# A hybrid attention layer on one core: the ALiBi slope folded into q's norm weights, and the softmax rows divided on GpSimd

## The chip, the cores and the metric

The kernel runs on one core of a Trainium2 chip. The metric is the device time of one execution in microseconds (us). A core has five engines with a queue of instructions each: TensorE (PE in the profile, its weight loads PEld), VectorE (DVE), ScalarE (ACT), GpSimd (POOL) and SyncE (SP, which here only issues DMAs). Each engine runs its queue in order; between engines semaphores set the order. SBUF is the on-chip memory of 128 partitions, PSUM the accumulator memory that TensorE writes; GpSimd works on SBUF alone.

## The reference

One decoder layer on 512 tokens of width 1024. Two token mixers work side by side, then come an MLP and a gated embedding. The change touches the second mixer, softmax attention with 8 heads of 128. Queries and keys are normalised per head (`rms_norm` with a weight vector each), and a penalty that grows with the distance is taken from the scores:

```
slopes = 2.0 ** (-8.0 * arange(1, H + 1) / H)          # H = 8: 2^-1 ... 2^-8
qh = rms_norm(mq, moba_q_norm)
kh = rms_norm(mk, moba_k_norm)
sc = einsum('qd,kd->qk', qh, kh) * dh ** -0.5 - slope * abs(t - pos)
prob = softmax(where(visible, sc, -inf))
out = prob @ vh
```

With 512 tokens and blocks of 256 keys, a query sees all keys up to itself. The rest of the layer is: a gated linear attention (4 heads), output gates for both mixers, `x = x + y @ w_out`, an MLP with squared ReLU (4096 hidden features), and a gated per-layer embedding.

## The kernel before, in words

Activations stand feature-major, [128 features, 512 tokens]; weights are the stationary operand. A float32 product is three passes of TensorE on exact halves, hi*hi + hi*lo + lo*hi (`mm3`, lines 101 to 103). So each operand is split: ScalarE copies the high half, and VectorE or GpSimd subtracts it for the low half (`split`, L91 and L92, and `halves`, L151 and L153). Weights come in units of 512 KB by DMA and are split the same way: `whi` by ScalarE, `wlo` by VectorE at L153.

The program is written in the order of issue. The projections are cut into ticks of 12 matmuls. Work of the attention heads runs as generators in the background: at each tick every generator that is due emits one stage, which thus goes into each engine's queue between the projections' instructions. A `yield n` puts the next stage n ticks later, `yield 0` later in the same tick. Nothing reorders the queues afterwards.

The projection of queries and keys has 16 tiles of 128 features, q and k of 8 heads in turn, so a head takes four ticks. The result of a tile is scaled into `e` (L417) and normalised by `qk_norm`: squares and their split (ScalarE, and GpSimd at L403 for the low half `ql`), their mean over the partitions by TensorE (L275, L276), the inverse root by ScalarE and VectorE (L286, L287), then e times weight times root (L408, weight `gq` or `gk`), and the split of the result with its low half on GpSimd (L153 on POOL).

Five ticks after k, `attention` begins for the head: the slope times the distances (L425, tile `s`), the split of the values (GpSimd, L92), the scores of four tiles of 128 queries against 128, 256, 384 or 512 keys (TensorE, 1280 columns in all). `lower` (L441) turns a tile of scores in PSUM to slope * distance - score in SBUF and takes the minimum of each row; `soften` is the exponential with the row's sum on ScalarE (L445); `normalise` takes the reciprocal of the sum (L448) and multiplies the row by it (L449). One tick or two later TensorE transposes the rows (L475), which are split again (L486 on ScalarE, L491 or L153 on VectorE), and multiplied with the values into `ob`.

After the 16 tiles comes a short projection for the low-rank gate, whose result VectorE reads at L526, and the gated linear attention. Two PSUM banks (`acc`) take turns for the projections, six (`aux`) for the rest.

Of the kernel before, what the change touches and what calls it, by code (L numbers as in the profile page):

```python
"""Hybrid decoder layer on one NeuronCore: MoBA attention and gated linear attention in parallel,
gated branches, a squared-ReLU MLP and a gated per-layer embedding.

Activations are kept feature-major ([feature, token]), so that each projection is
out^T = W^T act^T with W as the stationary operand; only the two value projections are
token-major.  A float32 product runs as three fp32r products of exact halves: the tensor engine
carries 12 significant bits, x = hi + lo with both halves exact, and hi*hi + hi*lo + lo*hi.
The RMS factor of a token commutes with the projection that follows and is applied to its output.

The program is in the order of issue.  The projections are cut into ticks of 12 matmuls; the work  # L10
of the attention heads runs in the background as generators that emit a stage per tick, each
stage fed by stages of earlier ticks, so that the tensor engine finds its operands ready.
"""
# [14 lines left out]
P = 128  # L28
# [9 lines left out]
# columns of the packed per-feature vectors  # L38
C_MIX, C_MLP, C_PLE, C_ON, C_Q, C_K, C_B, NCOL = 0, 8, 16, 24, 32, 33, 34, 38

# feature-major tiles of w_in in the order of use: (q, k) of each MoBA head, (q, k) of each GLA
# head, then g_r, gate_a and gate_b
# [4 lines left out]
def kernel(ctx: ExitStack, tc: tile.TileContext, xT, pT, w_in, w_val, w_glr, w2, cols,  # L47
# [41 lines left out]
    def split(hi, lo, src, eng=None):  # L89
        """hi + lo = src, exactly."""  # L90
        A.activation(hi, src, AF.Copy)  # L91
        (eng or V).tensor_tensor(lo, src, f32(hi), ALU.subtract)  # L92

    def scaled_split(hi, lo, x, g):
        """hi + lo = x * g, g a column."""
        A.activation(hi, x, AF.Copy, scale=g)  # L96
        V.scalar_tensor_tensor(lo, x, g, f32(hi), ALU.mult, ALU.subtract)

    def mm3(ps, a, b, start=True, stop=True):
        """ps (+)= a^T b from exact halves a = (hi, lo), b = (hi, lo)."""  # L100
        PE.matmul(ps, a[0], b[0], start=start, stop=False)  # L101
        PE.matmul(ps, a[0], b[1], start=False, stop=False)  # L102
        PE.matmul(ps, a[1], b[0], start=False, stop=stop)  # L103

# [1 line left out]
    jobs = []  # L106

    def spawn(gen, wait=0):
        """gen yields the number of ticks until its next stage; 0 is later in the same tick, when
        the others' stages of the tick have been issued."""  # L110
        jobs.append([gen, wait])
# [43 lines left out]
    def low_rank(g1, g2, raw):  # L155
        # The low-rank gate takes two passes: its columns come in pairs of groups of 16, the
        # first for hi*hi + hi*lo and the second for lo*hi.  Their sum is left to the product
        # with w2, where three pairs carry hi*hi, lo*hi and hi*lo in one pass.
        g1, g2 = (g.rearrange("p k (n c) -> p k n c", c=16) for g in (g1, g2))
        for i in range(0, 8, 2):  # L160
            A.activation(g1[:, :, i], raw, AF.Copy)
            A.activation(g2[:, :, i], raw, AF.Copy)
        yield 0
        for i in range(0, 8, 2):
            V.tensor_tensor(g1[:, :, i + 1], raw, f32(g1[:, :, i]), ALU.subtract)
            V.tensor_scalar(g2[:, :, i + 1], raw, 0.0, None, ALU.mult)
# [13 lines left out]
    def gemm_fm(n, act, evac, nu=1):  # L180
        """n tiles of 128 output features, [128 features, 512 tokens], each over nu units of
        [128, 8 k-tiles, 128]; act(k) are the halves of the activations' k-tile."""
        for i in range(n):
            ps = bank(accp, "acc")
            for u in range(nu):
                w = ready.pop(0)
                for half in range(2):
                    for k in range(4 * half, 4 * half + 4):
                        mm3(ps, (w[0][:, k], w[1][:, k]), act(8 * u + k),
                            u == 0 and k == 0, u == nu - 1 and k == KT - 1)  # L190
                    if half:
                        convert()
                    tick()
            evac(i, ps)

    def gemm_tm(act, evac, first=None):
        """512 output features, [128 tokens, 512 features] for each of the four tiles of tokens,
        over four units of [128, 2 k-tiles, 512]."""
        ps = [bank(accp, "acc"), bank(accp, "acc"), bank(), bank()]
        for u in range(4):  # L200
            w = first(u) if first else ready.pop(0)
            order = [(k, m) for k in range(2) for m in range(NT)]
            if u == 3:
                order = [(k, m) for m in range(NT) for k in range(2)]
            for j, (k, m) in enumerate(order):
                a = act(2 * u + k)
                ms = slice(m * P, (m + 1) * P)
                mm3(ps[m], (a[0][:, ms], a[1][:, ms]), (w[0][:, k], w[1][:, k]),
                    u == 0 and k == 0, u == 3 and k == 1)
                if j == 3 or j == 7:  # L210
                    if j == 7:
                        convert()
                    tick()
                if u == 3 and k == 1:
                    evac(m, ps[m])
# [33 lines left out]
    # the tensor engine's clock rises with use: keep it busy until the first operands are in  # L249
# [6 lines left out]
    # distance of query p of a tile to key j, counted from the first key that tile 3 sees;  # L256
    # beyond any score where the key lies ahead
# [5 lines left out]
    gq = const.tile([P, 1], F32, name="gq")  # L263
# [3 lines left out]
    def gains():  # L267
        V.tensor_scalar(gq, col[:, C_Q:C_Q + 1], 0.5 * QSCALE, None, ALU.mult)
        V.tensor_scalar(gk, col[:, C_K:C_K + 1], -0.5, None, ALU.mult)
        V.tensor_scalar(gon, col[:, C_ON:C_ON + 8], -0.5, None, ALU.mult)  # L270

    def mean_sq(sh, sl, n):
        """Bank whose every row holds the sum over the partitions of sh + sl, over n."""
        ps = bank()
        PE.matmul(ps, ones[n], sh, start=True, stop=False)  # L275
        PE.matmul(ps, ones[n], sl, start=False, stop=True)  # L276
        return ps

    def rsqrt_m2(ps):
        """-2 (ps + eps)^-0.5, an estimate from exp and ln with one Newton step."""  # L280
# [9 lines left out]
    def norm_end(r, s):  # L290
        """r = rsqrt(mean + eps) from the sums of squares s."""
# [100 lines left out]
    # ---- MoBA: two blocks of keys, of which a query sees its own causally and all of the one  # L392
    # before, so that the selection is the whole past ----
# [20 lines left out]
    def qk_evac(i, ps):  # L414
# [3 lines left out]
        spawn(qk_norm(hd, e, gk if isk else gq, 2 * isk))  # L418
# [3 lines left out]
    def attention(hd):  # L422
        qh, ql, kh, kl = (qk[hd][:, i] for i in range(4))
        ali = tt("s")
        V.tensor_scalar(ali, dist, 2.0 ** -(hd + 1), None, ALU.mult)  # L425
# [9 lines left out]
        def lower(i, sc):  # L435
            # t = slope * distance - score: the softmax of -t
# [4 lines left out]
            V.tensor_tensor_reduce(t, sc, ali[:, T - n:], 1.0, 3e38, ALU.add, ALU.min, mn)  # L441
# [5 lines left out]
        def normalise(t, mn, sm):  # L447
            V.reciprocal(sm, sm)  # L448
            V.tensor_scalar(t, t, sm, None, ALU.mult)  # L449
# [87 lines left out]
    def gla_gate(hd):  # L537
        """The decays of a head, [128, 4, 512]: from the middle of the chunk to the query and
        from the key to the middle, from the chunk's start to the query, from the key to its end;
        and the decay of the whole chunk."""  # L540
# [7 lines left out]
        # log_sigmoid(z) = min(z, 0) - ln(1 + exp(-|z|))  # L548
# [51 lines left out]
    def gla(hd):  # L600
# [17 lines left out]
        # keep the sources s <= c  # L618
# [212 lines left out]
    def ple_last(w):  # L831
        """The last tile, in two halves of the tokens."""
# [17 lines left out]
def _columns(w):  # L850
    """[K, N] -> [N / 128, K / 1024, 128, 8, 128]: units of 128 columns over eight k-tiles."""
# [5 lines left out]
def _rows(w):  # L857
    """[K, N] -> [N / 512, K / 256, 128, 2, 512]: units of 512 columns over two k-tiles."""
# [53 lines left out]
```

## Time and profile before

Three runs took 989.24, 988.56 and 987.33 us, median 988.56. One further execution was profiled; its span from the first to the last instruction is its own time as far as the profile has it.

| | us |
|---|---|
| median of three runs | 988.56 |
| span of the profiled execution | 987.9 |
| TensorE busy in it | 971.7 |
| VectorE busy | 546.3 |
| ScalarE busy | 433.1 |
| GpSimd busy | 75.9 |

The attention's softmax work (L441 to L449) runs from 83.3 to 218.2 us of the span. Busy means that the engine had an instruction under way, which includes the time in which that instruction itself was held up. Matmuls overlap with one another in the records.

### The profile page before, as it was taken

How to read it: one execution, taken by the hardware profiler on the slowest of the kernel's cores; microseconds unless marked ns; L12 is line 12 of the kernel's file. 1: busy time of each engine (PE TensorE's matmuls, PEld its weight loads, DVE VectorE, ACT ScalarE, POOL GpSimd, SP SyncE). 2: the span in 40 equal slices, each digit the busy share in tenths (PEclk: the TensorE clock that was granted, in tenths of full speed). 3: DMA queues.
4: the chain of work that ended last, by engine and by line, in shares of the span. 5: the costliest groups of instructions: out<-in, count | busy, mean ns of one | idle time of the engine just before them, and what ended most of it. 6: DMA issues, size and time to landing. Idle time of an engine off the chain costs nothing.

```text
span 987.9 us, 11295 instructions
## 1 busy us (share of the span) xinstructions
PE 971.7 (98%) x4424; PEld 806.0 (82%) x4424; DVE 546.3 (55%) x767; ACT 433.1 (44%) x657; POOL 75.9 (8%) x61
## 2 busy tenths in 40 slices
PE   9999999899999999999999999999999999999998
PEld 7888777687888888888888888888888888888886
DVE  5469999977546773333355555443233544344364
ACT  5558777757224852222223354432112434233441
POOL 0025333300222000000000000000000000000000
PEclk9999999899999999999999999999999999999999
DMA  7221111112221233234323223323323232323231
GB/s 256 86 85 64 64 57 48 60 64 86 87 81 47 65 106 104 92 103 171 107 86 106 86 86 107 107 86 107 107 86 113 99 103 90 107 86 106 86 128 43
DMA packets 26981, 92.83 MB, mean 94 GB/s; under 512 B 3120, under 2 KB 3504, under 8 KB 26672
## 3 DMA queue, kind: packets, MB, share of 16 engines
q1 hardware_dynamic: 26784, 92.09, 28.0%
q8 instruction: 35, 0.57, 0.2%
q14 instruction: 18, 0.15, 0.1%
q10 hardware_dynamic: 144, 0.02, 0.0%
HBM read 90.00 MB, written 2.10 MB: 93 GB/s over the span
## 4 chain that ended last, share of the span: by engine, by line
PE 88%; DVE 9%; issue 2%; ACT 1%; POOL 0%; DVEq 0%; POOLq 0%
PE acc L101 27%; PE acc L103 26%; PE acc L102 26%; PE aux L102 2%; PE aux L103 2%; PE aux L101 2%; DVE c L449 1%; DVE c L441 1%; DVE a L491 1%; DVE wlo L153 1%; PE aux L642 1%; DVE y L287 1%; DVE s L425 1%; DVE w L286 1%; DVE e L417 1%
## 5 line engine op out<-in xcount | busy, mean ns | idle before, releaser
L101 PE MATMUL acc<-a,whi 128*128 128x512 f32 x1088 | 425.5, 391 | 0.0
L102 PE MATMUL acc<-a,whi 128*128 128x512 f32 x1088 | 423.7, 389 | 0.0
L103 PE MATMUL acc<-a,wlo 128*128 128x512 f32 x1088 | 423.6, 389 | 0.0
L153 DVE TENSOR_TENSOR wlo<-raw,whi 128x1024 fp32r<-128x1024 f32 x160 | 205.1, 1282 | 112.3 <-ACT whi L151 110.8
L103 PEld LDWEIGHTS acc<-a,wlo 128*128 128x128 f32 x1088 | 204.2, 188 | 43.0
L101 PEld LDWEIGHTS acc<-a,whi 128*128 128x128 f32 x1088 | 204.3, 188 | 42.0
L102 PEld LDWEIGHTS acc<-a,whi 128*128 128x128 f32 x1088 | 204.3, 188 | 42.0
L151 ACT ACTIVATE whi<-raw 128x1024 fp32r<-128x1024 f32 x160 | 167.8, 1050 | 132.8 <-PE acc L102 109.1
L764 ACT ACTIVATE e<-e 128x512 f32<-128x512 f32 x32 | 20.2, 632 | 96.2 <-DVE e L756 92.9
L92 DVE TENSOR_TENSOR a<-e,a 128x512 fp32r<-128x512 f32 x40 | 27.7, 692 | 47.2 <-ACT a L91 47.2
L96 ACT ACTIVATE a<-c,col 128x512 fp32r<-128x512 f32 x16 | 11.6, 723 | 68.2 <-DVE c L770 42.3
L756 DVE SCALAR_TENSOR_TENSOR e<-acc,R 128x512 f32<-128x512 f32 x31 | 21.4, 691 | 34.6 <-PE acc L103 34.6
L770 DVE TENSOR_TENSOR c<-acc,c 128x512 f32<-128x512 f32 x16 | 11.1, 692 | 53.2 <-PE acc L103 53.2
L91 ACT ACTIVATE a<-e 128x512 fp32r<-128x512 f32 x40 | 25.3, 632 | 32.6 <-DVE e L725 31.6
L702 ACT ACTIVATE a<-a 128x512 f32<-128x512 f32 x16 | 10.1, 632 | 61.5 <-DVE a L701 61.5
L101 PE MATMUL acc<-c,whi 128*128 128x512 f32 (+1 forms) x82 | 31.8, 388 | 0.1
L102 PE MATMUL acc<-c,whi 128*128 128x512 f32 (+1 forms) x82 | 31.5, 384 | 0.0
L103 PE MATMUL acc<-c,wlo 128*128 128x512 f32 (+1 forms) x82 | 31.5, 384 | 0.0
L403 POOL TENSOR_TENSOR ql<-q,qh 128x512 fp32r<-128x512 f32 x16 | 22.6, 1415 | 110.1 <-ACT qh L401 110.1
L286 DVE SCALAR_TENSOR_TENSOR w<-aux,w 128x512 f32<-128x512 f32 x23 | 15.7, 684 | 23.3 <-ACT w L284 23.3
L101 PE MATMUL acc<-whi,a 128*128 128x512 f32 x64 | 25.9, 405 | 2.7 <-DVE e L526 2.7
L701 DVE TENSOR_TENSOR a<-acc,R 128x512 f32<-128x512 f32 x16 | 11.1, 691 | 29.0 <-PE acc L103 29.0
(177 smaller groups left out, 1030.6 us busy)
## 6 DMA issues: line engine op xcount, KB each, us to landing
raw<-in_w_in_dram SPq DMA_DIRECT2D x48, 512.0 KB, 3.3
raw<-in_w_up_dram SPq DMA_DIRECT2D x32, 512.0 KB, 3.3
raw<-in_w_down_dram SPq DMA_DIRECT2D x32, 512.0 KB, 3.3
raw<-in_w_val_dram SPq DMA_DIRECT2D x14, 512.0 KB, 3.3
raw<-in_w_a_dram SPq DMA_DIRECT2D x8, 512.0 KB, 3.3
raw<-in_w_b_dram SPq DMA_DIRECT2D x8, 512.0 KB, 3.2
raw<-in_w_out_dram SPq DMA_DIRECT2D x8, 512.0 KB, 3.3
raw<-in_w_gate_dram SPq DMA_DIRECT2D x8, 512.0 KB, 3.4
```

The source lines that it names most:

```text
L91: A.activation(hi, src, AF.Copy)
L92: (eng or V).tensor_tensor(lo, src, f32(hi), ALU.subtract)
L96: A.activation(hi, x, AF.Copy, scale=g)
L101: PE.matmul(ps, a[0], b[0], start=start, stop=False)
L102: PE.matmul(ps, a[0], b[1], start=False, stop=False)
L103: PE.matmul(ps, a[1], b[0], start=False, stop=stop)
L151: A.activation(hi, src, AF.Copy)
L153: (eng or V).tensor_tensor(lo, src, f32(hi), ALU.subtract)
L286: V.scalar_tensor_tensor(w, ps, EPS, w, ALU.add, ALU.mult)
L403: G.tensor_tensor(sl, q2, f32(sh), ALU.subtract)
L756: V.scalar_tensor_tensor(e, ps, 0.0, R1, ALU.max, ALU.mult)
L764: A.activation(e, e, AF.Square)
```

## The change

Queries get the inverse of the slope: head hd's weight vector is multiplied by 2^(hd+1) beside the constant it had, so `gq` has a column for each head, made by eight small VectorE instructions in place of one. The instruction of `lower` then adds the plain distances and multiplies the sum by 2^-(hd+1), in the place where its factor was 1.0. The tile of slope times distances (L425) is no longer made. In `normalise` the reciprocal stays on VectorE, and the multiplication goes to GpSimd, written with a second factor of 1.0. The comments are taken out of the file too, and lines move by up to three.

```diff
-    gq = const.tile([P, 1], F32, name="gq")
+    gq = const.tile([P, MH], F32, name="gq")
...
     def gains():
-        V.tensor_scalar(gq, col[:, C_Q:C_Q + 1], 0.5 * QSCALE, None, ALU.mult)
+
+        for hd in range(MH):
+            V.tensor_scalar(gq[:, hd:hd + 1], col[:, C_Q:C_Q + 1], 0.5 * QSCALE * 2.0 ** (hd + 1), None,
+                            ALU.mult)
...
-        spawn(qk_norm(hd, e, gk if isk else gq, 2 * isk))
+        spawn(qk_norm(hd, e, gk if isk else gq[:, hd:hd + 1], 2 * isk))
...
     def attention(hd):
         qh, ql, kh, kl = (qk[hd][:, i] for i in range(4))
-        ali = tt("s")
-        V.tensor_scalar(ali, dist, 2.0 ** -(hd + 1), None, ALU.mult)
...
-            V.tensor_tensor_reduce(t, sc, ali[:, T - n:], 1.0, 3e38, ALU.add, ALU.min, mn)
+            V.tensor_tensor_reduce(t, sc, dist[:, T - n:], 2.0 ** -(hd + 1), 3e38, ALU.add, ALU.min, mn)
...
         def normalise(t, mn, sm):
             V.reciprocal(sm, sm)
-            V.tensor_scalar(t, t, sm, None, ALU.mult)
+            G.tensor_scalar(t, t, sm, 1.0, ALU.mult, ALU.mult)
```

VectorE's queue in the stage of a head in which three tiles of rows are divided, the kernel before. `c` is the tile of rows, `sm` the sums and their reciprocals, `wlo` the low half of the next weights, `a` the low half of a transposed block.

```order
L448 RECIPROCAL sm_1466<-sm_1466 128x1
L449 TENSOR_SCALAR c_285_1464<-c_285_1464,sm_1466 128x512
L448 RECIPROCAL sm_1469<-sm_1469 128x1
L449 TENSOR_SCALAR c_285_1464<-c_285_1464,sm_1469 128x384
L448 RECIPROCAL sm_1472<-sm_1472 128x1
L449 TENSOR_SCALAR c_285_1464<-c_285_1464,sm_1472 128x128
L153 TENSOR_TENSOR wlo_1511<-raw_1322,whi_1510 128x1024
```

The same place in the changed kernel.

```order
L449 RECIPROCAL sm_1463<-sm_1463 128x1
L449 RECIPROCAL sm_1466<-sm_1466 128x1
L449 RECIPROCAL sm_1469<-sm_1469 128x1
L153 TENSOR_TENSOR wlo_1508<-raw_1321,whi_1507 128x1024
L510 TENSOR_TENSOR qh_1358<-q_258_1357,qh_1358 32x512
L153 TENSOR_TENSOR a_278_1454<-aux_1458,a_278_1454 128x256
```

The three reciprocals now stand in a row, and the subtraction for the weights follows them at once.

VectorE's queue where a head's q is normalised (L408 with `gq`) and the next head's attention begins, the kernel before.

```order
L287 SCALAR_TENSOR_TENSOR y_1376<-w_1377,y_1376 128x512
L408 SCALAR_TENSOR_TENSOR y_1376<-e_1252,gq,y_1376 128x512
L425 TENSOR_SCALAR s_1418<-dist 128x512
L153 TENSOR_TENSOR wlo_1403<-raw_1214,whi_1402 128x1024
L153 TENSOR_TENSOR a_61_466<-aux_1361,a_60_465 128x512
L417 TENSOR_TENSOR e_1442<-acc_1345,R_113 128x512
```

The same place in the changed kernel.

```order
L290 SCALAR_TENSOR_TENSOR y_1375<-w_1376,y_1375 128x512
L411 SCALAR_TENSOR_TENSOR y_1375<-e_1251,gq,y_1375 128x512
L153 TENSOR_TENSOR wlo_1402<-raw_1215,whi_1401 128x1024
L153 TENSOR_TENSOR a_61_473<-aux_1360,a_60_472 128x512
L420 TENSOR_TENSOR e_1439<-acc_1344,R_113 128x512
```

The instruction on the distances has gone from between q's last multiplication and the subtraction for the weights.

GpSimd's queue over one head, the kernel before. `ql` is the low half of the squares, `c` with `y` the low half of q or k, `v` that of the values.

```order
L153 TENSOR_TENSOR c_151_871<-y_814,c_151_871 128x512
L403 TENSOR_TENSOR ql_921<-q_167_919,qh_920 128x512
L153 TENSOR_TENSOR c_151_871<-y_914,c_151_871 128x512
L403 TENSOR_TENSOR ql_1006<-q_181_1004,qh_1005 128x512
L92 TENSOR_TENSOR v_190_1043<-a_12_143,v_190_1043 128x512
```

The same head in the changed kernel, with `sm` in the four new rows.

```order
L153 TENSOR_TENSOR c_149_874<-y_819,c_149_874 128x512
L406 TENSOR_TENSOR ql_924<-q_165_922,qh_923 128x512
L450 TENSOR_SCALAR c_155_903<-c_155_903,sm_905 128x512
L450 TENSOR_SCALAR c_155_903<-c_155_903,sm_908 128x384
L450 TENSOR_SCALAR c_155_903<-c_155_903,sm_911 128x128
L153 TENSOR_TENSOR c_149_874<-y_917,c_149_874 128x512
L450 TENSOR_SCALAR c_155_903<-c_155_903,sm_956 128x256
L406 TENSOR_TENSOR ql_1009<-q_179_1007,qh_1008 128x512
L92 TENSOR_TENSOR v_187_1044<-a_12_143,v_187_1044 128x512
```

Three multiplications stand ahead of k's low half, and the fourth between it and the next `ql`.

## Rows read from the trace of the kernel before

**Rows 1.** The page: span, and busy time of each engine.

```profile
span 987.9 us, 11295 instructions
...
PE 971.7 (98%) x4424; PEld 806.0 (82%) x4424; DVE 546.3 (55%) x767; ACT 433.1 (44%) x657; POOL 75.9 (8%) x61
```

**Rows 2.** Windows: from:to, length, busy us per engine, PE clock, DMA share, GB/s.

```profile
117.51:135.45 17.94, 17.38 (x88) 14.34 (x87) 17.52 (x34) 13.97 (x28) 7.05 (x5) 1.00 0.18 60
189.00:207.00 18.00, 16.58 (x70) 13.86 (x71) 13.25 (x31) 9.04 (x20) 2.59 (x2) 0.81 0.19 59
```

**Rows 3.** Waits of TensorE, 80 to 207 us: total us, times, longest.

```profile
PE aux L102 <- DVE a L153: 3.7, 5, 1.3
PE acc L101 <- DVE e L526: 2.7, 1, 2.7
PE aux L101 <- DVE mn L441: 2.3, 5, 1.4
```

**Rows 4.** Timeline of TensorE: start, duration, instruction, [idle before it, releaser].

```profile
126.55 0.39 PE L102 MATMUL aux<-a,v 128*128 128x256 f32 x1 [0.38 <-DVE a L153]
...
136.19 0.39 PE L101 MATMUL aux<-c 128*128 128x256 f32 x1 [0.16 <-DVE mn L441]
...
187.06 0.40 PE L102 MATMUL acc<-wlo,a 128*128 128x512 f32 x1
187.29 0.39 PE L103 MATMUL acc<-whi,a 128*128 128x512 f32 x1
190.42 0.79 PE L101 MATMUL acc<-whi,a 128*128 128x512 f32 x1 [2.74 <-DVE e L526]
```

**Rows 5.** Instruction groups of VectorE: count, busy us, mean ns, idle before.

```profile
L449 DVE TENSOR_SCALAR c<-c,sm 128x512 f32<-128x512 f32 (+3 forms) x32 | 18.2, 568 | 1.1
L425 DVE TENSOR_SCALAR s<-dist 128x512 f32<-128x512 f32 x8 | 9.9, 1240 | 0.0
```

**Rows 6.** Timeline of VectorE in one head, and one division later.

```profile
123.38 1.25 DVE L449 TENSOR_SCALAR c<-c,sm 128x384 f32<-128x384 f32 x1
...
124.94 1.22 DVE L153 TENSOR_TENSOR wlo<-raw,whi 128x1024 fp32r<-128x1024 f32 x1
...
130.58 1.51 DVE L425 TENSOR_SCALAR s<-dist 128x512 f32<-128x512 f32 x1
132.01 2.32 DVE L153 TENSOR_TENSOR wlo<-raw,whi 128x1024 fp32r<-128x1024 f32 x1
...
136.74 1.34 DVE L491 TENSOR_TENSOR a<-aux,a 128x512 fp32r<-128x512 f32 x3
...
197.75 0.42 DVE L449 TENSOR_SCALAR c<-c,sm 128x384 f32<-128x384 f32 x1
```

**Rows 7.** Timeline of GpSimd in the same head.

```profile
123.07 1.35 POOL L153 TENSOR_TENSOR c<-y,c 128x512 fp32r<-128x512 f32 x1 [2.71 <-ACT c L151]
...
130.45 1.36 POOL L92 TENSOR_TENSOR v<-a,v 128x512 fp32r<-128x512 f32 x1 [0.34 <-ACT v L91]
131.77 1.48 POOL L153 TENSOR_TENSOR c<-y,c 128x512 fp32r<-128x512 f32 x1
137.00 1.30 POOL L403 TENSOR_TENSOR ql<-q,qh 128x512 fp32r<-128x512 f32 x1 [3.75 <-ACT qh L401]
```

**Rows 8.** Instruction groups of GpSimd, by shape: dearest and cheapest of 512 columns.

```profile
L596 POOL TENSOR_TENSOR c<-c,e 128x512 f32<-128x512 f32 x8 | 14.1, 1764 | 85.7 <-ACT whi L151 53.9 <-DVE e L594 31.7
...
L619 POOL TENSOR_SCALAR_AFFINE_SELECT v<-v 128x512 f32<-128x512 f32 x4 | 2.8, 704 | 9.3 <-ACT v L616 9.3
```

**Rows 9.** Timeline of TensorE at the transposes and the scores.

```profile
130.00 1.04 PE L475 MATMUL aux<-ident,c 128*128 128x128 f32 x8
...
131.11 0.39 PE L102 MATMUL aux<-c 128*128 128x512 f32 x1
```

**Rows 10.** The instruction that makes q's weights: ns min/median/max, start.

```profile
L268 DVE TENSOR_SCALAR gq<-col x1: 143/143/143, 19.6 to 19.6; 128x1 f32<-128x1 f32 x1
```

## The prediction, made before the changed kernel ran

> **What bounds the kernel now.** I read the busy shares first, then the windows, then TensorE's waits, then the single waits in order of time, then VectorE's instructions in one attention head.
>
> The page puts TensorE at 98% of the span and VectorE at 55% [rows 1], which reads as if VectorE didn't matter. The windows say otherwise for one stretch. One head of the MoBA attention lies between 117.51 and 135.45 us, 17.94 us, and in it VectorE is busy for 17.52 us [rows 2]. So the share of 55% is an average over a stretch where VectorE is full and a long rest where it is half idle. All of the change lies in the full stretch.
>
> TensorE's waits between 80 and 207 us all end on VectorE: 3.7 us in 5 waits for the low half that L153 writes, 2.3 us in 5 for the minimum that L441 writes, and 2.7 us in one wait for L526's result. That is 8.7 us in 11 waits [rows 3]. Each costs more than its idle time, because the records of back-to-back matmuls overlap. L102 and L103 start at 187.06 and 187.29, 0.23 us apart, and the next start is 190.42, 3.13 us later. So 3.13 - 0.23 = 2.90 us are lost where the view shows 2.74 [rows 4], or 0.16 us more per wait. Eleven waits come to 8.7 + 1.8 = 10.5 us. Two of them belong to each ordinary head: 0.38 and 0.16 idle [rows 4], 0.86 us with the correction, so TensorE alone would need 17.94 - 0.86 = 17.1 us for a head.
>
> Then the clock. Between 189 and 207 us the mean granted clock is 0.81 [rows 2]: 0.19 x 18 x 2 = 6.8 us at 1.2 GHz in place of 2.4, after TensorE had stood still for 2.74 us. At most half of that, 3.4 us, is lost; some of it lies inside the wait itself, so I take 2.5. Together 10.5 + 2.5 = 13.0 us hang on VectorE being late. That is the whole that this change can win.
>
> **What the change removes.** L425, the multiplication of the distances by the slope, is gone: 8 instructions, 9.9 us. L449, the division of the rows, leaves VectorE: 32 instructions, 18.2 us [rows 5]. Per head that is (9.9 + 18.2) / 8 = 3.5 us of VectorE's 17.52, leaving 14.0.
>
> Not all of the 3.5 is work. Where nothing is beside it, a division of 384 columns takes 0.42 us; at 123.38 it takes 1.25, and the GpSimd instruction that started at 123.07 runs until 124.42 [rows 6, 7]. L425 takes 1.51 us at 130.58, beside the GpSimd instruction of 130.45 to 131.81. The same happens to the subtraction of two SBUF tiles in L153: 1.22 us at 124.94, 2.32 at 132.01, beside GpSimd's 131.77 to 133.25. An instruction fed from PSUM is not held: L491's three at 136.74 run for 1.34 us through a GpSimd instruction that starts at 137.00 [rows 6, 7]. At 0.42 us for 384 columns, the 512 + 1280 columns that leave in a head are 1.96 us of work, and the other 1.55 are waits for GpSimd. Those may be inherited: in both places the instruction that now comes next is L153's subtraction, which is one that waits. With all of it inherited VectorE has 14.0 + 1.55 = 15.6 us per head.
>
> **What it adds.** Four multiplications per head on GpSimd, 1280 columns. The trace has no such instruction there. The nearest rows for 512 columns are the one-input selection, 0.70 us, and above it two-input instructions, 1.35 in the attention and 1.76 in the gated part [rows 7, 8]. In proportion to columns a head costs 1.8, 3.4 or 4.4 us. I take 1.8, because the new instruction reads one tile, and keep 4.4 as the upper end. GpSimd is busy for 7.05 us of a head's 17.94 [rows 2], so even 7.05 + 4.4 = 11.5 us fits.
>
> Their wait: each needs the sum that ScalarE has left and a reciprocal that VectorE still makes. Behind the first three in GpSimd's order stand k's low half, then the fourth, then the next ql. K's low half now starts at 123.07 [rows 7] and the score matmul that reads it in its second pass at 131.11; the transposes of the normalised rows start at 130.00 [rows 9]. So about 130.0 - 123.0 = 7.0 us are there for the four multiplications and 1.35 us of k: 1.8 + 1.35 = 3.2 us at my price, 4.4 + 1.35 = 5.8 at the highest. It is hidden under TensorE's projections at all three prices; the cover ends at (7.0 - 1.35) / 2.5 = 2.3 us for 512 columns.
>
> The added wait for the port: the L153 subtraction that follows the three reciprocals can meet one multiplication already begun, up to 0.7 us. After that VectorE's next instructions read PSUM and don't wait. So a head is 15.6 + 0.7 = 16.3 us on VectorE, under TensorE's 17.1. Its bounds are 14.0 (nothing inherited, nothing met) and 15.6 + 4.4 = 20.0 (everything dear and waited for).
>
> The Trainium skill (SBUF — State Buffer, Who interferes with whom) says that a VectorE instruction with two SBUF inputs, or in a mode that uses both of its ports, and a GpSimd instruction that reads SBUF exclude each other for the whole of the one that began. By that rule the moved work is not free for VectorE: the sum would be 16.3 us if one piece is met and 15.6 + 1.8 = 17.4 if all are; this trace agrees with the rule (1.25 for 0.42, 1.34 unmoved).
>
> Edits with no price of their own: the slope as the factor of L441's instruction, which has a factor (1.0) now already; seven more multiplications of 128x1 in the first projection, 7 x 0.14 = 1.0 us at most [rows 10], before any attention; the distances read in place of their copy.
>
> **The sum.** TensorE becomes the later engine in an ordinary head, and its waits for VectorE go. I don't count all 13.0. Half of the longest L441 wait (1.4), 0.7, may stay, since VectorE is late there before the first division has left it. Half of the longest L153 wait (1.3), 0.7, because L509 stays in that place. And 1.1 of the 2.74 before the gated part, because L153 and L526 stand one behind the other there. 13.0 - 2.5 = 10.5 us. The profiled span is 987.9 us, its forecast 977.4; the median of the three runs is 988.56, 0.66 above that span, and 988.56 - 10.5 = 978.1. I predict 978.
>
> **Rivals.**
> 1. *VectorE waits for every new GpSimd instruction (slower).* The place is the pair reciprocal and L153 in each head: if the port isn't given back between the multiplications, VectorE stands until all are through. At 3.4 us a head is 15.6 + 3.4 = 19.0 us, 1.06 over today's 17.94, in (207 - 80) / 17.94 = 7 heads: 988.6 + 7.4 = 996. It decides from 17.94 - 15.6 = 2.3 us of new waiting per head. For it: L153's 2.32 us. Against it: L425 got through at 132.09 while a GpSimd instruction had already begun at 131.77 [rows 6, 7], so the two alternate.
> 2. *The normalised rows are late at the transposes (no change).* With 2.6 us for 512 columns GpSimd needs 2.5 x 2.6 + 1.35 = 7.9 us of the 7.0, and TensorE waits 0.9 us per head for GpSimd in place of 0.86 for VectorE; with all else as it is, 988.6. Against it: no row is dearer than 1.76.
>    The Trainium skill (GPSIMD Engine Reference, Engine selection) advises against GpSimd for arithmetic on a tile, as about half as fast with two inputs and near VectorE's rate with one; no run shows the latter for a multiplication.
> 3. *Half of it.* VectorE's work comes in bursts inside a head, so half of the ten waits for L441 and L153 stay (3.7 + 2.3 + 10 x 0.16 = 7.6 us, of which 3.8 are won), and the wait before the gated part stays with its low clock: 988.6 - 3.8 = 984.8. For it: the reciprocals and L153 still stand ahead of the low half that TensorE waits for. Against it: that half would come some 2 us earlier than the 126.55 at which TensorE now goes on [rows 4], by the division that has gone from the same place.
>
> **How the numbers follow.** The forecast has 0.62, with a range of its own of 974.5 (all 13.0 and 1 more) to 982; half of it 0.16; no change 0.12; slower 0.10. A measurement here tells about 0.2% from no change, 2 us. Faster: 0.62 + 0.16 = 0.78; same 0.12; slower 0.10. The range of eight in ten leaves out rival 1 and the outer ends: 974 to 988.
>
> **What would show it.** Right: VectorE's busy time in a head falls from 17.52 to 14 to 16.5; the rows of waits for L441 and L153 shrink to under 2 us together; a head takes 17.0 to 17.3 us; the granted clock stays at 1.0 between 189 and 207 us; the new GpSimd instruction of 512 columns takes 0.6 to 1.0 us; after 240 us nothing differs. Wrong: L153 longer than 2.3 us behind the reciprocals in each head (rival 1), transposes that wait for GpSimd (rival 2), or the wait before the gated part unchanged (rival 3). If the new instruction costs over 2.3 us for 512 columns, the forecast falls.

## The result, and the profile after

The changed kernel takes 975.87 us (median of 4 runs, 975.58 to 976.03) against 988.9 us (987.33 to 989.59, 4 runs) on the same chip, a ratio of 0.9872, interval 0.9858 to 0.9886. That is 13.0 us less; 10.5 were forecast, 978 with a range of 974 to 988.

The page of the changed kernel. VectorE's share of the span has hardly moved [rows 1], from 55% to 54%, so the share shows nothing of what happened; GpSimd has 30 us more.

```profile
span 973.8 us, 11302 instructions
...
PE 966.3 (99%) x4424; PEld 804.1 (83%) x4424; DVE 522.1 (54%) x734; ACT 431.7 (44%) x657; POOL 105.9 (11%) x93
```

The window of one head of the changed kernel, from one head's first score matmul to the next, answers to [rows 2]: from:to, length, busy us of each engine, PE clock. TensorE is now without a gap, 16.84 of 16.84 us, and VectorE has 2.4 us to spare. The second row, 180 to 207 us, shows a granted clock of 1.00; before, 189 to 207 us had 0.81.

```profile
110.88:127.72 16.84, 16.84 (x90) 14.35 (x88) 14.44 (x28) 13.86 (x29) 10.63 (x10) 1.00 0.20 63
...
180.00:207.00 27.00, 26.86 (x137) 22.65 (x136) 18.81 (x48) 18.68 (x41) 9.71 (x10) 1.00 0.18 60
```

The waits of TensorE over the whole span of the changed kernel. The eleven waits of [rows 3] are gone. The first row is the start of the program; the last three lie at 213 and 221 us, in the gated part.

```profile
PE aux L252 <- DVE ones L248: 2.2, 1, 2.2
PE aux L102 <- DVE a L153: 0.4, 1, 0.4
PE aux L476 <- DVE a L153: 0.3, 1, 0.3
PE aux L543 <- DVE a L585: 0.2, 1, 0.2
```

VectorE's own waits between 82 and 190 us say who was late. The kernel before has no row there: VectorE stood for nobody in this whole stretch. The changed kernel has these, and a third row of 0.2 us: VectorE now waits for ScalarE, and in the ordinary heads for TensorE's scores.

```profile
DVE w L289 <- ACT w L287: 5.1, 10, 0.6
DVE c L442 <- PE aux L103: 2.6, 3, 0.9
```

The chain of waits says the same from the other end. First the shares of the kernel before, then those of the changed one: VectorE's 9% of the chain are TensorE's now.

```profile
PE 88%; DVE 9%; issue 2%; ACT 1%; POOL 0%; DVEq 0%; POOLq 0%
```

```profile
PE 97%; DVE 1%; ACT 1%; issue 0%; POOL 0%; POOLq 0%
```

Where the time came from is shown by one matmul that both programs have, the gated part's second one for the decays (L542 before, L543 after), in each kernel's timeline.

```profile
212.41 0.47 PE L542 MATMUL aux<-ql,qh 128*128 128x512 f32 x1
```

```profile
198.29 0.47 PE L543 MATMUL aux<-ql,qh 128*128 128x512 f32 x1
```

It comes 14.1 us earlier, and the two profiled spans differ by 987.9 - 973.8 = 14.1 us. So all of the gain lies ahead of this point, in the attention and the first tick behind it. It can be parted once more. The seventh head's first score matmul starts at 184.73 us before and at 176.42 after: 8.3 us come from the waits ahead of it. The 88 matmuls from there to the eighth head's first score matmul take 5.8 us less. Before, the wait of 2.74 us and the low clock behind it lie in this window.

```profile
184.73:207.10 22.37, 19.63 (x88) 16.22 (x87) 17.62 (x34) 13.12 (x28) 5.53 (x5) 0.85 0.15 48
```

```profile
176.42:192.99 16.57, 16.57 (x88) 14.17 (x87) 11.26 (x27) 11.77 (x26) 8.80 (x8) 1.00 0.19 65
```

VectorE and GpSimd in one head of the changed kernel (start, duration, instruction; idle before it) show who now waits for whom.

```profile
119.06 1.66 DVE L153 TENSOR_TENSOR wlo<-raw,whi 128x1024 fp32r<-128x1024 f32 x1
...
123.83 1.67 DVE L411 SCALAR_TENSOR_TENSOR y<-e,gq,y 128x512 f32<-128x512 f32 x1
125.42 1.21 DVE L153 TENSOR_TENSOR wlo<-raw,whi 128x1024 fp32r<-128x1024 f32 x1
```

```profile
118.95 0.70 POOL L450 TENSOR_SCALAR c<-c,sm 128x512 f32<-128x512 f32 x1 [1.07 <-DVE sm L449]
...
119.62 1.55 POOL L450 TENSOR_SCALAR c<-c,sm 128x384 f32<-128x384 f32 x1
...
121.49 1.31 POOL L153 TENSOR_TENSOR c<-y,c 128x512 fp32r<-128x512 f32 x1
122.76 0.49 POOL L450 TENSOR_SCALAR c<-c,sm 128x256 f32<-128x256 f32 x1
...
125.52 2.26 POOL L92 TENSOR_TENSOR v<-a,v 128x512 fp32r<-128x512 f32 x1 [0.57 <-ACT v L91]
```

The multiplication of 512 columns takes 0.70 us, as the one-input selection of [rows 8]. VectorE's subtraction at 119.06 meets it and waits until it is through; then the 384 columns on GpSimd wait for the subtraction (1.55 us; 0.59 where nothing is beside them). In q's tick it is now GpSimd's v that waits (2.26 us against 1.36 in [rows 7]), while VectorE's subtraction takes its free 1.21 where it took 2.32 [rows 6].

### The profile page after: what moved, and what is told of

It is laid out like the page before. It is cut to its first block, busy times and chain, and to the rows that moved or that the text cites. A ratio compares the mean times of both kernels' runs of the same rounds, so it can differ in the third digit from the quotient of the medians.

```text
span 973.8 us, 11302 instructions
## 1 busy us (share of the span) xinstructions
PE 966.3 (99%) x4424; PEld 804.1 (83%) x4424; DVE 522.1 (54%) x734; ACT 431.7 (44%) x657; POOL 105.9 (11%) x93
## 4 chain that ended last, share of the span: by engine, by line
PE 97%; DVE 1%; ACT 1%; issue 0%; POOL 0%; POOLq 0%
PE acc L101 29%; PE acc L102 28%; PE acc L103 28%; PE aux L102 2%; PE aux L103 2%; PE aux L101 2%; PE aux L476 1%; PE aux L643 1%; PE aux L278 1%; PE aux L646 1%; PE aux L279 1%; PE aux L630 1%; PE aux L252 0%; PE aux L611 0%; DVE a L829 0%; PE acc L521 0%
## 5 line engine op out<-in xcount | busy, mean ns | idle before, releaser
L102 PE MATMUL acc<-a,whi 128*128 128x512 f32 x1088 | 423.7, 389 | 0.0
L153 DVE TENSOR_TENSOR wlo<-raw,whi 128x1024 fp32r<-128x1024 f32 x160 | 203.5, 1272 | 112.8 <-ACT whi L151 110.8
L102 PEld LDWEIGHTS acc<-a,whi 128*128 128x128 f32 x1088 | 204.3, 188 | 41.9
L102 PE MATMUL acc<-c,whi 128*128 128x512 f32 (+1 forms) x82 | 31.5, 384 | 0.0
L289 DVE SCALAR_TENSOR_TENSOR w<-aux,w 128x512 f32<-128x512 f32 x23 | 15.9, 691 | 28.5 <-ACT w L287 28.4
L450 POOL TENSOR_SCALAR c<-c,sm 128x512 f32<-128x512 f32 (+3 forms) x32 | 26.5, 839 | 18.9 <-DVE sm L449 18.9
L285 ACT ACTIVATE y<-aux,epsc 128x512 f32<-128x512 f32 x23 | 15.8, 685 | 26.8 <-PE aux L279 26.6
```

The source lines that it names most:

```text
L289: V.scalar_tensor_tensor(w, ps, EPS, w, ALU.add, ALU.mult)
L450: G.tensor_scalar(t, t, sm, 1.0, ALU.mult, ALU.mult)
```

## Experiments

Two theories stood against each other. Theory 1: a head costs the larger of TensorE's own time and VectorE's, and the change took VectorE below TensorE. Theory 2: the loss was the collisions between VectorE and GpSimd, where an instruction of one stands until one of the other is through, and the change ended them. All medians below are beside runs of the kernel before on the same chip, 989.1 to 989.4 us.

### Each part by itself

The slope alone leaves the division on VectorE:

```diff
-            G.tensor_scalar(t, t, sm, 1.0, ALU.mult, ALU.mult)
+            V.tensor_scalar(t, t, sm, None, ALU.mult)
```

> The slope is folded as in the change, the division stays on VectorE. Theory 1 (a head costs the larger of TensorE's 16.83 us and VectorE's own time, and the change took VectorE below TensorE): VectorE's head was 17.52 us, L425 takes 1.24 out of it, so 16.3 to 17.0 if the next subtraction inherits part of its wait; the waits for L441 and L153 mostly go, 977 to 981 us, clock 1.0 between 180 and 200 us. Theory 2 (the loss was the collision between the division and GpSimd on their common port): nearly all of the loss stays, 985 to 989 us.

Measured: 980.04 us, ratio 0.9904 (0.9888 to 0.9921).

The division alone is the kernel before with its L449 on GpSimd:

```diff
-            V.tensor_scalar(t, t, sm, None, ALU.mult)
+            G.tensor_scalar(t, t, sm, 1.0, ALU.mult, ALU.mult)
```

> The division is on GpSimd as in the change, the slope tile L425 is still made on VectorE. Theory 1: 17.52 - 2.28 = 15.2 us of VectorE per head, under 16.83: 975.5 to 978 us. Theory 2: the divisions collide no more, also 976 to 979, but with L425 at 1.5 us beside GpSimd. A third theory, that only both parts together bring VectorE under TensorE, expects 982 to 987 here and in the run with the slope alone.

Measured: 977.35 us, ratio 0.9877 (0.9862 to 0.9892).

So the parts win 9.3 and 12.0 us by themselves, and 13 together: far from additive. One ordinary head of each, the slope alone and then the division alone, shows why.

```profile
128.05:144.89 16.84, 16.84 (x89) 14.35 (x88) 16.42 (x32) 13.85 (x29) 7.78 (x6) 1.00 0.16 52
```

```profile
111.66:128.50 16.84, 16.84 (x89) 14.35 (x88) 15.91 (x29) 13.74 (x29) 12.46 (x11) 1.00 0.20 63
```

VectorE has 16.42 and 15.91 us, both under 16.84, and the head takes TensorE's 16.84 in both. Once below, further relief buys nothing in an ordinary head. What the whole change adds lies where a head isn't ordinary. With the slope alone one of them has VectorE above 16.84 again, and is longer:

```profile
144.89:162.49 17.60, 17.13 (x90) 14.35 (x88) 17.12 (x34) 14.45 (x36) 7.38 (x5) 1.00 0.19 61
```

Two rows of TensorE's waits with the slope alone (0.4 us of the first lies at 226 us, in the gated part):

```profile
PE aux L102 <- DVE a L153: 2.1, 3, 1.3
PE acc L101 <- DVE e L527: 1.3, 1, 1.3
```

The wait before the gated part is 1.3 us here, 1.0 with the division alone, and gone with both. In neither did the clock fall behind it (1.00 from 176 to 190 us), so the clock's part of the gain comes with either half. The third theory, that it takes both parts, is out.

### Work on VectorE that does not collide

To part the two theories, the changed kernel got work on VectorE that reads no SBUF: fills of a scratch tile behind each reciprocal. Nothing else changes; `k` is 1, 2 or 3.

```diff
+    fill = const.tile([P, P], F32, name="fill")
...
             G.tensor_scalar(t, t, sm, 1.0, ALU.mult, ALU.mult)
+            for _ in range(k * (t.shape[1] // P)):
+                V.memset(fill, 0.0)
```

> The changed kernel with work on VectorE that reads nothing: after each reciprocal one fill of a 128x128 scratch tile per 128 columns of the row tile, ten per head, about 0.21 us each (as the 128-column L442 instructions are spaced), 2.1 us per head. Theory 1: 14.43 + 2.1 = 16.5 us per head, still under 16.83: within 2 us of the changed kernel, 975 to 978 us. Theory 2: nothing, 976.

Measured: 977.77 us, ratio 0.9881 (0.9867 to 0.9896).

> The changed kernel with twice the fills of the first dose (20 per head). In the run with three doses a fill took 0.245 us from start to start, so 4.9 us per head: VectorE 14.4 + 4.9 = 19.3 us against TensorE's 16.84. Theory 1 (the larger of the two sets the head): 2.5 to 3.2 us per head over 7.5 heads, 994 to 1000 us, the waits on L153 are back. Theory 2 (collisions on the port alone): at most 980.

Measured: 999.11 us, ratio 1.0104 (1.0089 to 1.0119).

> The same with three times the fills, 6.3 us per head on VectorE, none of which reads SBUF. Theory 1: VectorE 20.7 us per head, 3.9 over TensorE's 16.83, in 7 heads 27 us, and the waits for L441, L153 and L526 and the low clock are back: 998 to 1006 us. Theory 2 (collisions with GpSimd, not VectorE's time): no SBUF is read, so no more than 3 us over the changed kernel, up to 979.

Measured: 1028.39 us, ratio 1.0394 (1.0378 to 1.0409).

GpSimd isn't held by the fills: its 512 columns take 0.69 us beside twelve of them. Nor are the fills: all 240 with three doses take 0.165 us each.

```profile
131.44 3.01 DVE L453 MEMSET fill<- 128x128 f32 x12
131.57 0.69 POOL L451 TENSOR_SCALAR c<-c,sm 128x512 f32<-128x512 f32 x1 [1.07 <-DVE sm L450]
```

Theory 2 falls as the whole account: by fills, which don't collide, the kernel gets 23 and 52 us slower than the changed one. So VectorE's time counts, whatever it is spent on. The collisions are part of that time, though. In the head before, L449's 384 columns, L408 for q, L425 and the second L153 took 1.25, 1.67, 1.51 and 2.32 us. Where nothing holds them up, the first, second and fourth take 0.42, 0.75 and 1.22 [rows 6 and below]; for L425 I take the 0.49 of L449's 512 columns. The difference is 3.9 us, an estimate, and without it VectorE's 17.52 would be 13.6, below 16.84. No run kept the work and took only the collisions out.

```profile
121.58 0.75 DVE L408 SCALAR_TENSOR_TENSOR y<-e,gk,y 128x512 f32<-128x512 f32 x1
122.78 0.49 DVE L449 TENSOR_SCALAR c<-c,sm 128x512 f32<-128x512 f32 x1
128.98 1.67 DVE L408 SCALAR_TENSOR_TENSOR y<-e,gq,y 128x512 f32<-128x512 f32 x1
```

Theory 1 has the shape (one dose nearly free, two and three not), but its size for three doses was missed by some 22 us. Two heads with two doses, then one with three:

```profile
94.76:117.12 22.36, 19.23 (x90) 15.41 (x88) 20.41 (x49) 15.42 (x32) 12.82 (x12) 0.92 0.15 53
117.12:135.11 17.99, 17.13 (x90) 14.33 (x88) 16.07 (x47) 13.07 (x27) 9.79 (x9) 1.00 0.17 58
```

```profile
123.51:146.80 23.29, 19.71 (x89) 16.39 (x88) 20.34 (x59) 13.85 (x29) 10.59 (x10) 0.85 0.14 45
```

TensorE waits 2.62 us in the first of these heads and 3.58 in the third, and its granted clock falls, to 0.92 and 0.85 as means of the head. With three doses it waits 30.0 us in 8 waits for L153. But the low clock isn't what was missed, because VectorE sets the head. Its waits from 82 to 219 us with three doses are one row, with none for TensorE:

```profile
DVE w L290 <- ACT w L288: 1.0, 2, 0.5
```

So the slow matmuls ran beside a VectorE that never waited for them. What was missed is the size of VectorE's own head. A fill counts as 0.165 us busy, but the next starts 0.245 us later. Thirty fills are thus 7.4 us where the expectation had 6.3, which makes 14.4 + 7.4 = 21.8. Measured from one head's first L443 to the next, it is:

```profile
125.12:147.89 22.77, 19.19 (x84) 15.86 (x83) 19.82 (x58) 13.86 (x28) 10.06 (x10) 0.85 0.14 47
```

Without the fills' 30 x 0.165 us VectorE is busy for 14.9 of it, 0.5 more than in the changed kernel; the rest is short gaps. Six such heads, 82.00 to 219.71 us, have a mean of 22.95, 6.1 over 16.84 where the expectation had 3.9.

### More work on GpSimd

The second rival was that the rows come late at the transposes. Here every tile is multiplied again by 1.0, once, twice or three times more:

```diff
             G.tensor_scalar(t, t, sm, 1.0, ALU.mult, ALU.mult)
+            for _ in range(n - 1):
+                G.tensor_scalar(t, t, 1.0, 1.0, ALU.mult, ALU.mult)
```

> The changed kernel with each row tile multiplied twice on GpSimd (the second time by 1.0): 1.4 us for 512 columns, 2.1 us more per head, and up to 0.8 us of waits for VectorE on the port, half of the 1.6 us that the run with three multiplications showed. 2.9 us is less than the 3.7 us between the fourth multiplication and the transposes in the changed kernel: hidden, 975 to 978, no wait of L478 for GpSimd. If the cover is shorter than that (the run with three cost 27 us where 4 were expected), 981 to 990.

Measured: 986.27 us, ratio 0.9969 (0.9958 to 0.9981).

> The changed kernel with each row tile multiplied three times on GpSimd (the second and third time by 1.0), 3 x 0.70 = 2.1 us for 512 columns, 4.3 us more per head, GpSimd 10.6 + 4.3 = 14.9 of 16.84 us. The prediction's cover of 2.3 us for 512 columns: hidden, 975 to 978. By the changed kernel's own trace the fourth multiplication ends at 123.25 and the transposes start at 126.92, 3.7 us later: 4.3 - 3.7 = 0.6 us late per head, TensorE waits for GpSimd, about 4 us over the changed kernel, 979 to 982.

Measured: 1003.03 us, ratio 1.0146 (1.0128 to 1.0163).

> The same with four multiplications, 2.8 us for 512 columns, 6.4 us more per head: GpSimd 17.0 us of 16.84, full, and the rows late at the transposes by 6.4 - 3.7 = 2.7 us per head. The prediction's second rival (the rows late at the transposes) at its price: TensorE waits for GpSimd at L476, 2 to 3 us per head in 7 heads, 990 to 999 us. If instead GpSimd's work is hidden whatever it costs, 975 to 978.

Measured: 1023.13 us, ratio 1.0342 (1.0325 to 1.0359).

The two expectations with three and four multiplications were far too low. The third, on record after their results, had 975 to 978 first and 981 to 990 as the other case, which came true. GpSimd and TensorE in one head with two multiplications per tile:

```profile
121.72 0.69 POOL L450 TENSOR_SCALAR c<-c,sm 128x512 f32<-128x512 f32 x1 [1.07 <-DVE sm L449]
122.50 1.46 POOL L452 TENSOR_SCALAR c<-c 128x512 f32<-128x512 f32 x1
...
125.82 1.84 POOL L153 TENSOR_TENSOR c<-y,c 128x512 fp32r<-128x512 f32 x1
127.64 1.98 POOL L450 TENSOR_SCALAR c<-c,sm 128x256 f32<-128x256 f32 x1
129.70 0.40 POOL L452 TENSOR_SCALAR c<-c 128x256 f32<-128x256 f32 x1
```

```profile
130.16 0.55 PE L478 MATMUL aux<-ident,c 128*128 128x128 f32 x3 [0.19 <-POOL c L452]
```

From the first multiplication to the end of the last it is 130.10 - 121.72 = 8.4 us, where the changed kernel needs 123.25 - 118.95 = 4.3. The second multiplications are 1.9 us of that. Most of the rest is waiting for VectorE: 1.98 for 0.49, 1.46 for 0.62, 1.84 for 1.31. In this head the longer GpSimd work meets VectorE's L153 and both L411, and each of these holds it up in turn. So the transposes at 130.16 wait 0.19 us in an ordinary head, and others 2.3 and 2.8 us, at 95.7 and 183.1 us; the six waits are 6.0 us.

With three multiplications TensorE waits in nearly every head, and the clock follows. The row for its waits, the transposes at which one ends, and four windows of 2 us around them:

```profile
PE aux L478 <- POOL c L452: 17.9, 9, 2.3
```

```profile
141.24 1.52 PE L478 MATMUL aux<-ident,c 128*128 128x128 f32 x7 [2.27 <-POOL c L452]
```

```profile
138.00:140.00 2.00, 0.97 (x5) 0.52 (x3) 0.88 (x2) 0.00 (x0) 1.92 (x4) 1.00 0.68 215
140.00:142.00 2.00, 0.76 (x5) 0.76 (x6) 0.00 (x0) 0.06 (x1) 1.83 (x4) 0.88 0.12 47
142.00:144.00 2.00, 2.00 (x8) 1.71 (x7) 0.00 (x0) 1.20 (x3) 2.00 (x3) 0.50 0.30 36
144.00:146.00 2.00, 2.00 (x11) 1.87 (x10) 1.34 (x5) 0.13 (x1) 0.90 (x1) 0.76 0.28 103
```

A wait of 2.3 us is followed by matmuls at half clock, and the head takes 21.2 us, 4.4 over 16.84. None of these three expectations had the clock in it.

### The next waits

The waits that are left lie in the gated part, where GpSimd has little to do (4.1 of the 25 us from 199 to 224). One of two subtractions there was moved to it, and run twice, the second time beside the changed kernel on one chip.

```diff
-        V.tensor_tensor(c3(el), B3, B3[:, :, P - 1:P].to_broadcast([P, NT, P]), ALU.subtract)
+        G.tensor_tensor(c3(el), B3, B3[:, :, P - 1:P].to_broadcast([P, NT, P]), ALU.subtract)
```

> The changed kernel with one more move: the second subtraction of the decays in the gated part (L562, four of 0.68 us, between 199 and 224 us) on GpSimd, which is idle there. TensorE's last waits for VectorE there come to about 1.8 us (213.06, 213.72, 221.38 and one at 198.3). If they hang on VectorE's time: 0.5 to 1.8 us faster than the changed kernel, 974 to 975.5. If ScalarE's exponentials then wait for GpSimd's slower subtraction, or VectorE's order in one tick sets them: no change, 975.5 to 976.5.

Measured: 975.39 us, ratio 0.9861 (0.9847 to 0.9876).

> The changed kernel itself, on the chip of the next run, so that the two can be compared: 975.5 to 976.5.

Measured: 975.57 us, ratio 0.9866 (0.9851 to 0.988).

> The changed kernel with L562's four subtractions on GpSimd once more, beside the changed kernel on the same chip. Its trace showed one of three late waits gone (0.54 us): 0.3 to 0.8 us faster, 975.0 to 975.5. If two kernels this near can't be told apart, the same.

Measured: 975.24 us, ratio 0.9861 (0.9846 to 0.9876).

Its first profile lacks the 0.4 us wait of L102 for L153 at 221 us, but 975.24 and 975.57 can't be told apart by these intervals. No version was shown to beat the changed kernel.

## Why the prediction was right, step by step

- *VectorE is full in the attention though its share is 55%, and TensorE waits for it.* Right. VectorE's waits show it, none before between 82 and 190 us, and the fills show that VectorE's time slows the kernel without a collision. The four ways below 16.84 us (the change, each half, one dose of fills) give ordinary heads of 16.84, or 0.2 more with the slope alone; the longer heads, 17.60 with the slope alone and 17.22 with one dose, are those in which VectorE has most to do.
- *TensorE alone needs 17.1 us per head.* 16.84 measured, below the 17.0 to 17.3 that was named as a sign. Each of a head's two waits cost (17.94 - 16.84) / 2 = 0.55 us, not 0.43: the 0.16 us added to a wait's idle time, read from one wait, was too little.
- *13.0 us hang on VectorE being late, of which 10.5 are won.* The first figure was near and the second too cautious. That the medians differ by 13.0 to the tenth is luck, since the four runs before lie 2.3 us apart. The profiled pair differs by 14.1. The ten waits ahead of the seventh head's scores are worth 8.3 us of that, where the prediction had 7.6, and the wait before the gated part with its low clock 5.8, where it had 2.9 + 2.5 = 5.4. The three remnants that were left in (0.7, 0.7 and 1.1 us) are not there. The half-removed versions show that such remnants exist, 1.3 and 1.0 us before the gated part, when VectorE has 16.4 or 15.9 us per head; with 14.4 it has caught up.
- *VectorE's head comes to 16.3 us.* This term was mis-sized: 14.44. I let all of the 1.55 us of waiting be inherited and added 0.7. Collisions are still there, 0.92 each in both L411 (1.67 for 0.75) and 0.45 in one L153, together 2.3 us. But L153 in q's tick no longer waits; being earlier, VectorE asks first, and GpSimd waits in its place.
- *Four multiplications cost GpSimd 1.8 us, as a one-input instruction does.* 0.70, 0.59, 0.48 and 0.37 us where nothing holds them up, 2.1 together, and 3.3 per head with their waits for VectorE (26.5 us for all 32). The choice of the one-input row was right for 512 columns; the narrow ones cost more than their columns.
- *The cover ends at 2.3 us for 512 columns.* Wrong, and it did not matter at 0.70. With two multiplications, 1.3 us for 512 columns, TensorE already waits and 10 us of the 13 are lost. The step counted GpSimd's instructions and not their waits for VectorE. That the work is hidden even at 4.4 us per head isn't borne out either: two multiplications per tile are 2.1 + 1.9 = 4.0, and TensorE waits. The second rival was thus nearer than I put it: its mechanism is the one that the added work on GpSimd showed, at about half the price that I gave.
- *The first rival (VectorE waits for every new GpSimd instruction).* Didn't happen: one of the four is met per head. The two engines alternate, as L425's end had suggested.
- *The low clock costs 2.5 us.* The clock is at 1.00 after the change, as expected. Of the 5.8 us the wait accounts for 2.9 by the prediction's correction, which leaves 2.9 for the clock; that is an estimate, as no run changed the clock alone. The run with three multiplications agrees in kind: 2.3 us of waiting made a head 4.4 us longer.

## What to carry to other kernels

A busy share over the whole span hides a stage in which an engine is full; read it in a window of one period, beside the period that the bounding engine would need alone. Relief counts only down to that second figure, so two edits that each get there don't add up. When work goes to GpSimd beside a busy VectorE, the cover must hold its waits for VectorE too, which here were as large as the work that was added.

## What the runs showed of the hardware

- A GpSimd multiplication by a column, float32 in SBUF: 0.70 us for 512 columns, 0.59 for 384, 0.48 for 256 and 0.37 for 128. By the first and the last that is about 0.26 us and 0.86 us per 1000 columns, an estimate.
- Fills on VectorE don't hold GpSimd: 0.69 us for 512 columns during the fills. A fill of 128x128 takes 0.165 us, but twelve in a row take 3.01, 0.245 from start to start.
- Which of the two engines waits depends on who asks first: VectorE's subtraction takes 1.66 us when it starts 0.11 behind a GpSimd instruction (119.06), and 1.21 when it starts 0.10 ahead of one (125.42). In the ordinary heads this changed in q's tick when VectorE got 3 us lighter: VectorE's 2.32 us became 1.21, and GpSimd's 1.36 became 2.26.
- TensorE stood 1.0 and 1.3 us with each half of the change, and 1.66 us once with three multiplications, with a granted clock of 1.00 in the 3 us behind the wait. Behind 2.27 us with three multiplications and 2.62 us with two doses of fills it was 0.55 and 0.66 as a mean, down to the lower level of 0.50. One wait of 2.33 us, with two multiplications, was followed by 1.00.
- What a fall of the clock costs depends on which engine is full. The 2.74 us wait before made the same 88 matmuls 5.8 us longer, and 2.27 us with three multiplications a head 4.4 us longer. With three doses of fills the clock was 0.86 for 138 us, and VectorE never waited for TensorE.
